# Down-projection of a gated MLP in column parts of 448 and 256 instead of 352 and 352, with the operand's rows closed up and moved by 64 bytes

## The chip, the cores and the metric

The kernel runs on one core of one Trainium2 chip. The metric is the device time of one execution in microseconds; the time given for a kernel is the median of several executions. TensorE (PE) multiplies, VectorE (DVE), ScalarE (ACT) and GpSimd (POOL) do the elementwise work, and SyncE (SP) issues most of the DMAs.

## The reference, cut to what matters

One layer of a streaming encoder for 2048 prompt tokens and 64 sample tokens, model width 1024. The first half is a normalised and modulated projection into a pooling mixer and a matrix-memory recurrence, an output projection and a residual. The second half is the one that is changed here:

```python
h2 = rmsnorm(x, g2) * (1 + sc2) + sh2
up = h2 @ w_up                                  # 1024 -> 2 * 2816
conv = b_conv + sum(w_conv[j] * upp[:, j:j + T] for j in range(3))
a, g = jnp.split(conv, 2, -1)
x = x + gt2 * ((jax.nn.silu(g) * a) @ w_down)   # 2816 -> 1024, the down-projection
y = rmsnorm(x, g_final)
```

All is float32.

## The kernel before, in words

Features lie on the 128 partitions and tokens along the free dimension, so a matmul has a 128x128 block of weights as its stationary operand and a row of tokens as its moving operand. To keep float32 accuracy, each operand is held as two float32r numbers, a rounded high part and the low rest. One product is three matmuls (`PASSES`, L401): high weights by high data, high weights by low data, low weights by high data. Every matmul loads its stationary block anew.

The attention half works in four groups of 512 tokens, the last of them with the 64 sample tokens added (576, in blocks of 256 and 320 columns). Its projections are the matmuls of L416 (data moves) and L970/L1039 (weights move, data stationary).

The MLP half works in three groups of 704 tokens (`fgroups`, `FT` = 704, `FH` = 352). The 22 blocks of 128 inner features are taken in four parts of 5, 5, 6 and 6 (`PARTS`). For each block the up-projection is made by a scheme of seven products on halves of 352 columns (`product`, L1438 to L1447; its matmuls are L1443). Then follow convolution, SiLU and gate, and the result `tg`, 128x704, is split into its high and low part: `split_hi` on ACT (L1558) writes the high part into a tile `av`, `split_lo` on DVE (L1566) the low rest behind it. The tile has 1536 columns.

When the blocks of one part are done, the down-projection of that part runs (`down`, L1699 to L1712, matmuls at L1704): for each of the 8 blocks n of 128 output features, and each block k of the part, three passes, and in each pass one matmul for every column part in `secs`. `down_end` (L1714) adds the sum, scaled, to the residual `x3` on DVE (L1719). There are 3 x 22 x 8 x 3 = 1584 such passes, with two matmuls each.

How `av` lies, before: in all but the last part of the last group ("apart") the tile holds four rows of 384 columns, of which 352 are used: high left, high right, low left, low right. So every moving row of 352 columns starts a multiple of 1536 bytes after the start of the tile. In the block with index 1 of each part the low right row is moved by `NUDGE` = 4 columns, and the split is written in two pieces for that. In the last part of the last group, the tile has two rows of 704, 768 columns apart. There the first three n use the halves 0 to 352 and 352 to 704, and the other five use `ENDS`, 0 to 448 for all five n and then 448 to 704 for all five n, so that the final norm of the first columns can begin early.

In the built program the buffers of streamed weights (`wt`) begin 96 bytes past a multiple of 256 bytes, and so does every 128x128 block in them. The tiles `av` begin 224 bytes past one. In the last part, the weights of the five last n lie in other buffers (`hx`), which begin 224 bytes past a multiple of 256. The data tiles of the attention half (`hl`, `mx`) hold their rows 160 bytes past one.

The order on PE, ACT, DVE and POOL is the program's in this half (a manual schedule); a list of small steps (`todo`, `tick`) puts the elementwise work of the next block between the matmuls. Weights come on SP's queue in the order in which they are used, some units ahead. Accumulators are six banks of PSUM taken in turn, two for each n.

Of the kernel before, what the change touches and what calls it, by code (L numbers as in the profile page):

```python
# [9 lines left out]
F32 = mybir.dt.float32  # L10
F32R = mybir.dt.float32r
AF = mybir.ActivationFunctionType
ALU = mybir.AluOpType
# [12 lines left out]
FT = 704  # L26
FH = FT // 2
NFG = NTOK // FT
NE = 3
EB = 1  # L30
ENDS = ((0, 448), (448, 704))
PARTS = ((0, 5), (5, 10), (10, 16), (16, 22))
EPS = 1e-6
HD = 128
# [7 lines left out]
XR = 384  # L42
XT = 4 * XR
NUDGE, NUDGED = 4, "T1"
# [15 lines left out]
def tile_layer(ctx: ExitStack, tc: tile.TileContext, xT, vecs, cst, rst, rowv, w_mod, w_ada, w_qkou, w_v, w_pool,  # L60
               w_out, w_up, w_down, st_C, st_pool, yT, o_pool, o_C, o_m, o_conv):
    nc = tc.nc
    act, dve, pool, pe = nc.scalar, nc.vector, nc.gpsimd, nc.tensor
# [30 lines left out]
    def scr():  # L94
        return sp.tile([P, TMAX], F32, tag="scr", name="scr")
# [59 lines left out]
    def pair_of(t, row, n):  # L155

        return t[:, :2 * row].rearrange("p (a t) -> p a t", a=2)[:, :, :n]
# [73 lines left out]
    for g in range(NG):  # L231
# [9 lines left out]
        for bi, (lo, hi) in enumerate(o.blks):  # L241
            for (a, b, s) in o.segs:
                l, h = max(lo, a), min(hi, b)
# [59 lines left out]
    for g in range(NFG):  # L303
        for (f0, f1_) in PARTS:
            late = []
# [7 lines left out]
            for i, (n, k) in enumerate(order):  # L313
# [3 lines left out]
                if k % 4 == 0 or (n, c) not in seen:  # L317
                    seen.add((n, c))
                    d = min(c + 4, f1_)
# [6 lines left out]
    class Unit:  # L326

        state = 0
        w = raw = None
# [460 lines left out]
    if True:  # L790
# [110 lines left out]
        h, pb = [], []  # L901
# [422 lines left out]
        for o in groups:  # L1324
# [15 lines left out]
            if o.g == 0:  # L1340
                dve.tensor_copy(M[:, GT + 1:GT + 2], RV[:, 2:3])
                dve.tensor_scalar(out=GH, in0=V[:, V_GH:V_GH + NH], scalar1=0.5, scalar2=None, op0=ALU.mult)
                t = scr()
                nc.sync.dma_start(out=t[:36, :512], in_=cst[:36, NCST + 512:NCST + 1024])
                dve.tensor_copy(E_r.rearrange("p h n -> p (h n)"), t[:36, :512])
                t = scr()
# [34 lines left out]
            h = hn  # L1381
# [74 lines left out]
    class Pair:  # L1456
# [85 lines left out]

        def split_hi(self):
            t = f2.tile([P, XT], F32R, tag="av", name="av", bufs=6)
            self.apart = not (self.o.last and self.f >= PARTS[-1][0])
            if self.apart:
                d = t.rearrange("p (a h t) -> p a h t", a=2, h=2)
                w = NUDGE if self.i == 1 else 0
                self.cuts = [(lambda b, i=i, pa=pa, pb=pb: d[:, b, i, pa + w * b * i:pb + w * b * i], a + 2 * s, b + 2 * s)
                             for (i, pa, pb, a, b, s) in self.o.pieces] if self.o.last or w else [  # L1550
                    (lambda b: d[:, b, :, :FH], 0, FT)]
                self.av[self.i] = lambda b, lo, hi: d[:, b, lo // FH, w * b * (lo // FH):w * b * (lo // FH) + hi - lo]
            else:
                d = pair_of(t, 2 * XR, FT)
                self.cuts = [(lambda b, lo=a, hi=e: d[:, b, lo:hi], a + 2 * s, e + 2 * s) for (a, e, s) in self.o.segs]
                self.av[self.i] = lambda b, lo, hi: d[:, b, lo:hi]
            for cut, a, b in self.cuts:
                act.activation(cut(0), self.of_tg(cut(0), a, b), AF.Copy)  # L1558

        def of_tg(self, like, a, b):  # L1560
            v = self.tg[:, a:b]
            return v.rearrange("p (h t) -> p h t", h=2) if len(like.shape) == 3 else v

        def split_lo(self):
            for cut, a, b in self.cuts:
                dve.tensor_tensor(out=cut(1), in0=self.of_tg(cut(0), a, b), in1=cut(0).bitcast(F32), op=ALU.subtract)  # L1566

    def reload(Bo):
        for nm in BN:
# [103 lines left out]
    for o in fgroups:  # L1673
        Bo = B[o.g]
        for pi, (f0, f1_) in enumerate(PARTS):
            nf = f1_ - f0
            lastp = pi == len(PARTS) - 1
            ends = o.last and lastp
# [51 lines left out]
                if ends:  # L1730
                    act.activation(x3[n][:, lo:hi], x3[n][:, lo:hi], AF.Copy, scale=V[:, V_GF + n:V_GF + n + 1])

            both = ((0, FH), (FH, FT))
            Ws = [Row() for _ in range(NE)]
            pss = []

# [19 lines left out]
            rows = {n: Row() for n in range(NE, KD)}  # L1756
            for secs in [(c,) for c in ENDS] if ends else (both,):
                sums = [(ssum, 0)]
# [94 lines left out]
```

## Time and profile before

| what | value |
|---|---|
| time, median of 3 runs | 2228.41 us (2227.61 to 2228.67) |
| profiled execution, its own time | 2224.26 us |
| its span, first to last instruction | 2222.5 us |
| mean granted TensorE clock | 0.996 |
| PE busy | 2193.2 us (99%) |
| DVE, ACT, POOL busy | 1572.3 us (71%), 1004.6 us (45%), 200.3 us (9%) |
| matmuls of L1443 (seven products) | 5544 |
| matmuls of L1704 (down-projection) | 3168 |

The busy time of an engine is the union of its instructions. A matmul's record shows when it starts and a modelled end; records overlap, because matmuls are pipelined. So the cost of one in a row of matmuls is read from the distance of their starts, which is the busy time of a row of them without gaps divided by their number, not from the mean duration. The chain of waits gives such stretches: "x264" beside a start and a length is a row of 264 matmuls on the path. A count in a window takes in each matmul that touches the window.

### The profile page before, as it was taken

The numbers are of one execution on the slowest core, as the hardware profiler recorded it, in microseconds if no ns is written. First come the engines' busy times: TensorE is split into PE (matmuls) and PEld (weight loads), VectorE is DVE, ScalarE is ACT, GpSimd is POOL, SyncE is SP. The second block draws the span as 40 slices with busy tenths as digits, with TensorE's granted clock in tenths as the row PEclk, the third lists the DMA queues.
The fourth block names the chain that finished last, engine by engine and source line by source line (L and its number), as shares of the span: only waits on it lengthen the run. The fifth ranks groups of instructions, "written<-read, shape, count | busy, mean of one in ns | idle before, by whom it ended". The sixth has DMA issues, their size and how long they took to land.

```text
span 2222.5 us, 37975 instructions
## 1 busy us (share of the span) xinstructions
PE 2193.2 (99%) x13726; PEld 2079.8 (94%) x13726; DVE 1572.3 (71%) x2906; ACT 1004.6 (45%) x1992; POOL 200.3 (9%) x475
## 2 busy tenths in 40 slices
PE   8999999999999999999999999999999999999998
PEld 6888888888899989999999999999999999999998
DVE  5877659567765778687858677677767685757474
ACT  4553334244333446465636344545445353445254
POOL 0010001001000101010000210000001210101012
PEclk9999999999999999999999999999999999999999
DMA  9968986997899476657656865556448554353442
GB/s 367 328 239 270 326 291 225 333 308 246 286 304 302 144 239 208 212 170 267 210 170 215 288 220 197 194 196 203 151 163 281 190 191 159 110 179 121 143 154 81
DMA packets 276444, 493.52 MB, mean 222 GB/s; under 512 B 24952, under 2 KB 103416, under 8 KB 276256
## 3 DMA queue, kind: packets, MB, share of 16 engines
q1 hardware_dynamic: 264480, 463.01, 62.8%
q10 hardware_dynamic: 11776, 28.09, 3.4%
q8 instruction: 108, 1.77, 0.3%
q14 instruction: 80, 0.66, 0.1%
HBM read 382.77 MB, written 108.22 MB: 221 GB/s over the span
## 4 chain that ended last, share of the span: by engine, by line
PE 59%; DVE 1%; DMA 1%; ACT 1%; issue 1%; POOL 0%; POOLq 0%; ACTq 0%; DVEq 0%
PE mm L1443 38%; PE mm L1704 21%; DMA raw<-w_down 1%; DMA wt<-wsum 0%; DVE tg L1431 0%; ACT tg L1426 0%; DVE wt L362 0%; DMA wt<-wsplit 0%; ACT wt L359 0%; DVE y L1656 0%; PE m L1599 0%; ACT av L1558 0%; DVE tg L1541 0%; DVE ta L1431 0%; DVE x L1719 0%
## 5 line engine op out<-in xcount | busy, mean ns | idle before, releaser
L1443 PE MATMUL mm<-hx,wt 128*128 128x352 f32 x5544 | 887.4, 321 | 5.2 <-DVE wt L362 2.7
L1443 PEld LDWEIGHTS mm<-hx,wt 128*128 128x128 f32 x5544 | 881.4, 188 | 6.9 <-DVE wt L362 2.9
L1704 PE MATMUL mm<-av,wt 128*128 128x352 f32 (+2 forms) x3168 | 509.7, 321 | 0.5 <-DVE av L1566 0.3
L1704 PEld LDWEIGHTS mm<-av,wt 128*128 128x128 f32 x3168 | 502.6, 188 | 3.9 <-DVE av L1566 0.9
L416 PE MATMUL mm<-hl,wt 128*128 128x512 f32 (+2 forms) x1920 | 398.2, 359 | 4.6 <-DMA wt<-hl_kept 2.2
L362 DVE TENSOR_TENSOR wt<-raw,wt 128x512 fp32r<-128x512 f32 (+3 forms) x494 | 307.1, 637 | 90.6 <-ACT wt L359 88.0
L416 PEld LDWEIGHTS mm<-hl,wt 128*128 128x128 f32 x1920 | 313.0, 188 | 54.0 <-issue 7.1
L359 ACT ACTIVATE wt<-raw 128x512 fp32r<-128x512 f32 (+3 forms) x494 | 271.4, 570 | 199.6 <-PE mm L1704 85.3
L416 PE MATMUL mm<-mx,wt 128*128 128x512 f32 (+1 forms) x960 | 187.4, 355 | 2.0 <-DVE wt L362 1.6
L1719 DVE SCALAR_TENSOR_TENSOR x<-mm,MOD,x 128x352 f32<-128x352 f32 (+4 forms) x224 | 106.5, 526 | 113.6 <-PE mm L1704 113.5
L416 PEld LDWEIGHTS mm<-mx,wt 128*128 128x128 f32 x960 | 160.2, 190 | 27.3 <-DVE wt L362 1.9
L1431 DVE SCALAR_TENSOR_TENSOR tg<-eg,V,tg 128x704 f32<-128x704 f32 (+1 forms) x132 | 125.7, 952 | 52.3 <-ACT tg L1426 49.9
L362 DVE TENSOR_TENSOR wt<-wt 128x512 fp32r<-128x512 f32 x176 | 121.8, 692 | 41.9 <-ACT wt L359 41.9
L359 ACT ACTIVATE wt<-wt 128x512 fp32r<-128x512 f32 x176 | 109.9, 626 | 66.8 <-DMA wt<-wsum 58.2
L1431 DVE SCALAR_TENSOR_TENSOR ta<-ea,V,ta 128x704 f32<-128x704 f32 (+1 forms) x132 | 125.7, 952 | 7.6 <-ACT ta L1426 5.1
L1566 DVE TENSOR_TENSOR av<-tg,av 128x704 fp32r<-128x704 f32 (+4 forms) x112 | 62.1, 588 | 45.5 <-ACT av L1558 45.2
L1537 ACT ACTIVATE tg<-tg 128x704 f32<-128x704 f32 (+1 forms) x66 | 52.4, 793 | 81.6 <-DVE tg L1431 75.9
L1491 ACT ACTIVATE u<-mm 128x352 f32<-128x352 f32 x66 | 30.5, 463 | 127.5 <-PE mm L1443 92.4
L1451 DVE TENSOR_TENSOR eg<-mm,u 128x352 f32<-128x352 f32 x154 | 70.2, 468 | 23.0 <-ACT u L1506 11.2
L196 DVE SCALAR_TENSOR_TENSOR acc<-raw,CA,acc 128x512 f32<-128x512 f32 x84 | 60.6, 745 | 32.8 <-DMA raw<-w_ada 32.8
L1039 PE MATMUL mm<-wt,hl 128*128 128x256 f32 (+1 forms) x576 | 70.9, 282 | 0.0
L1039 PEld LDWEIGHTS mm<-wt,hl 128*128 128x128 f32 x576 | 69.2, 188 | 1.0 <-issue 0.6
(280 smaller groups left out, 1947.7 us busy)
## 6 DMA issues: line engine op xcount, KB each, us to landing
wt<-hl_kept SPq DMA_DIRECT2D x108, 512.0 KB, 6.1
raw<-w_up SPq DMA_DIRECT2D x198, 256.0 KB, 3.8
wt<-wsum SPq DMA_DIRECT2D x176, 256.0 KB, 3.9
wt<-wsplit SPq DMA_DIRECT2D x88, 512.0 KB, 4.3
raw<-w_down SPq DMA_DIRECT2D x96, 256.0 KB, 3.4
w<-w_up SPq DMA_DIRECT2D x88, 256.0 KB, 5.5
wsum<-w SPq DMA_DIRECT2D x44, 512.0 KB, 4.8
wsplit<-wt SPq DMA_DIRECT2D x44, 512.0 KB, 4.2
```

The costliest lines, as they stand in the source:

```text
L196: dve.scalar_tensor_tensor(out=acc[s], in0=w, scalar=CA[:, k, s:s + 1], in1=acc[s], op0=ALU.mult, op1=ALU.add)
L359: act.activation(u.w[:, 0, :u.n], u.raw[:, :u.n], AF.Copy)
L362: dve.tensor_tensor(out=u.w[:, 1, :u.n], in0=u.raw[:, :u.n], in1=u.w[:, 0, :u.n].bitcast(F32), op=ALU.subtract)
L416: pe.matmul(ps[bi][:, :hi - lo], U[:, a, k % 4 * P:(k % 4 + 1) * P], mv[k][:, b, lo:hi], start=(at == 0 and pi == 0), stop=(k == order[-1] ...
L1039: pe.matmul(ps[ti][:n, :cols], h[4 * kh + k4][:, b, lo:lo + n], U[:, a, k4 % 2 * cols:(k4 % 2 + 1) * cols], start=(kh == 0 and k4 == 0 and ...
L1431: dve.scalar_tensor_tensor(out=t[:, :E], in0=ext[:, j:j + E], scalar=wc(j, f), in1=t[:, :E], op0=ALU.mult, op1=ALU.add)
L1443: pe.matmul(ps[:, :FH], U[:, a, kc * P:(kc + 1) * P], Bo.at(nm, kc, b), start=(first and kc == 0 and pi == 0), stop=(kc == 3 and pi == 2), ...
L1451: dve.tensor_tensor(out=ext[:, d:d + b - a], in0=ps[:, a:b], in1=u[:, a:b], op=ALU.add)
L1537: act.activation(self.tg[:, :E], self.tg[:, :E], AF.Silu)
L1566: dve.tensor_tensor(out=cut(1), in0=self.of_tg(cut(0), a, b), in1=cut(0).bitcast(F32), op=ALU.subtract)
L1704: pe.matmul(ps[i][:, :hi - lo], U[:, a, k % 4 * P:(k % 4 + 1) * P], av[k](b, lo, hi), start=(k == 0 and (a, b) == PASSES[0]), stop=(k == n ...
L1719: dve.scalar_tensor_tensor(out=x3[n][:, a:b], in0=ps[i][:, a - lo:b - lo], scalar=gt2(n, s), in1=x3[n][:, a:b], op0=ALU.mult, op1=ALU.add)
```

## The change

The two rows of `av` are written without a gap, the high part's 704 columns and then the low part's, from column `SIDE` = 16 (64 bytes) of the tile on, in all parts. The split is one piece on each engine, or two in the last group, where the 64 sample tokens follow a gap in `tg`. The down-projection uses the column parts 0 to 448 and 448 to 704 (`ENDS`) everywhere. The nudge in `av` is gone; that in the operand of the seven products stays.

A part of 448 columns is 1792 bytes and a row of 704 is 2816 bytes, both multiples of 256. So all four rows now start at the same place within 256 bytes: in the built program 32 bytes past a multiple, while the streamed weights keep their 96.

```diff
+SIDE = 16
         def split_hi(self):
             t = f2.tile([P, XT], F32R, tag="av", name="av", bufs=6)
-            self.apart = not (self.o.last and self.f >= PARTS[-1][0])
-            if self.apart:
-                d = t.rearrange("p (a h t) -> p a h t", a=2, h=2)
-                w = NUDGE if self.i == 1 else 0
-                self.cuts = [(lambda b, i=i, pa=pa, pb=pb: d[:, b, i, pa + w * b * i:pb + w * b * i], a + 2 * s, b + 2 * s)
-                             for (i, pa, pb, a, b, s) in self.o.pieces] if self.o.last or w else [
-                    (lambda b: d[:, b, :, :FH], 0, FT)]
-                self.av[self.i] = lambda b, lo, hi: d[:, b, lo // FH, w * b * (lo // FH):w * b * (lo // FH) + hi - lo]
-            else:
-                d = pair_of(t, 2 * XR, FT)
-                self.cuts = [(lambda b, lo=a, hi=e: d[:, b, lo:hi], a + 2 * s, e + 2 * s) for (a, e, s) in self.o.segs]
-                self.av[self.i] = lambda b, lo, hi: d[:, b, lo:hi]
+            d = t[:, SIDE:SIDE + 2 * FT].rearrange("p (a t) -> p a t", a=2)
+            self.cuts = [(lambda b, lo=a, hi=e: d[:, b, lo:hi], a + 2 * s, e + 2 * s) for (a, e, s) in self.o.segs]
+            self.av[self.i] = lambda b, lo, hi: d[:, b, lo:hi]
             for cut, a, b in self.cuts:
-                act.activation(cut(0), self.of_tg(cut(0), a, b), AF.Copy)
+                act.activation(cut(0), self.tg[:, a:b], AF.Copy)
...
         def split_lo(self):
             for cut, a, b in self.cuts:
-                dve.tensor_tensor(out=cut(1), in0=self.of_tg(cut(0), a, b), in1=cut(0).bitcast(F32), op=ALU.subtract)
+                dve.tensor_tensor(out=cut(1), in0=self.tg[:, a:b], in1=cut(0).bitcast(F32), op=ALU.subtract)
...
-            both = ((0, FH), (FH, FT))
+            both = ENDS
```

More of the change, by code (lines that the diff above doesn't have):

```diff
@@ L1544, in split_hi @@
             t = f2.tile([P, XT], F32R, tag="av", name="av", bufs=6)
-            self.apart = not (self.o.last and self.f >= PARTS[-1][0])
-            if self.apart:
-                d = t.rearrange("p (a h t) -> p a h t", a=2, h=2)
-                w = NUDGE if self.i == 1 else 0
-                self.cuts = [(lambda b, i=i, pa=pa, pb=pb: d[:, b, i, pa + w * b * i:pb + w * b * i], a + 2 * s, b + 2 * s)
-                             for (i, pa, pb, a, b, s) in self.o.pieces] if self.o.last or w else [
-                    (lambda b: d[:, b, :, :FH], 0, FT)]
-                self.av[self.i] = lambda b, lo, hi: d[:, b, lo // FH, w * b * (lo // FH):w * b * (lo // FH) + hi - lo]
-            else:
-                d = pair_of(t, 2 * XR, FT)
-                self.cuts = [(lambda b, lo=a, hi=e: d[:, b, lo:hi], a + 2 * s, e + 2 * s) for (a, e, s) in self.o.segs]
-                self.av[self.i] = lambda b, lo, hi: d[:, b, lo:hi]
+            d = t[:, SIDE:SIDE + 2 * FT].rearrange("p (a t) -> p a t", a=2)
+            self.cuts = [(lambda b, lo=a, hi=e: d[:, b, lo:hi], a + 2 * s, e + 2 * s) for (a, e, s) in self.o.segs]
+            self.av[self.i] = lambda b, lo, hi: d[:, b, lo:hi]
             for cut, a, b in self.cuts:
[L1558 to L1562, printed above, removed]
+                act.activation(cut(0), self.tg[:, a:b], AF.Copy)
         def split_lo(self):
             for cut, a, b in self.cuts:
-                dve.tensor_tensor(out=cut(1), in0=self.of_tg(cut(0), a, b), in1=cut(0).bitcast(F32), op=ALU.subtract)
+                dve.tensor_tensor(out=cut(1), in0=self.tg[:, a:b], in1=cut(0).bitcast(F32), op=ALU.subtract)
     def reload(Bo):
```

## The prediction

> **What bounds the kernel now.** I read the page's busy rows first, then the chain that ended last in order of time, then windows of single stretches, because only there is the cost of one matmul to be seen.
>
> ```profile
> PE 2193.2 (99%) x13726; PEld 2079.8 (94%) x13726; DVE 1572.3 (71%) x2906; ACT 1004.6 (45%) x1992; POOL 200.3 (9%) x475
> PEclk9999999999999999999999999999999999999999
> PE mm L1443 38%; PE mm L1704 21%; DMA raw<-w_down 1%; DMA wt<-wsum 0%; DVE tg L1431 0%; ACT tg L1426 0%; DVE wt L362 0%; DMA wt<-wsplit 0%; ACT wt L359 0%; DVE y L1656 0%; PE m L1599 0%; ACT av L1558 0%; DVE tg L1541 0%; DVE ta L1431 0%; DVE x L1719 0%
> L1704 PE MATMUL mm<-av,wt 128*128 128x352 f32 (+2 forms) x3168 | 509.7, 321 | 0.5 <-DVE av L1566 0.3
> ```
>
> PE is busy 99% of the span at the full granted clock. The down-projection, L1704, holds 509.7 us of PE and waits only 0.5 us in all of it. So the question is what one matmul costs when the next stands ready, and whether two parts of 448 and 256 columns cost more or less than two of 352. The chain gives the present cost. The columns are start, length and what ran:
>
> ```profile
> 1235.64 41.84 PE mm L1704 x264
> 2082.53 77.93 PE mm L1443 x492
> 2160.47 3.88 PE mm L1704 x24
> ```
>
> 41.84 us for 264 matmuls is 158.5 ns for one and **317.0 ns for a pair**. The seven products, also 352 wide, take 77.93 / 492 = 158.4 ns, with operands in the same place relative to the weights. But the 24 matmuls at the head of the last part, which lie in the other layout, take 161.7 ns: same width, same clock, another place, 3.2 ns more.
>
> **The change part by part.** (1) *The matmuls.* There are 1584 passes with a pair of matmuls each. 1440 of them run in the gapped layout. 54 (three n by six blocks by three passes of the last part) run 352 wide in the ungapped one. The last 90 already use 448 and 256. I call *offset* the distance, modulo 256 bytes, from the beginning of a weight block to that of the moving row: by the program's addresses it is 128 now in the 1440, mixed 128 and 0 in the 54, 0 in the 90, and 192 (32 minus 96) after the change in the first two, 64 (32 minus 224) in the 90. No row shows 448 columns at 192. The widths and offsets that the trace does show:
>
> ```profile
> 2180.00:2196.00 16.00, 16.00 (x81) 1.00 0.12 33
> L1704 PE MATMUL mm<-av,wt 128*128 128x448 f32 x90 | 18.4, 365 | 0.0
> L1704 PE MATMUL mm<-av,wt 128*128 128x256 f32 x90 | 11.5, 285 | 0.0
> 605.00:615.00 10.00, 10.00 (x90) 1.00 1.01 359
> L1039 PE MATMUL mm<-wt,hl 128*128 128x256 f32 x70 | 8.3, 276 | 0.0
> L1039 PE MATMUL m<-wt,hl 128*64 128x256 f32 x20 | 2.6, 276 | 0.0
> 766.00:795.00 29.00, 29.00 (x222) 1.00 0.83 274
> 363.00:397.00 34.00, 34.00 (x150) 1.00 0.81 273
> ```
>
> The first row is the stretch of 448 alone at offset 0 (the fourth column of these window rows is the granted clock, 1.00 in all); rows two and three are its whole groups by shape. In a group without gaps the busy time less one record's modelled length, over the number less one, is the step: 448 takes (18.4 - 0.365) / 89 = **202.6 ns**, and 256, in three stretches, (11.5 - 3 x 0.285) / 87 = **122.4 ns**. Both at offset 0; the pair would be 325.0.
>
> Row four is L1039, 256 columns at **offset 192** (there the streamed weights move and the data stands still; rows five and six say that the window holds nothing else): (10.00 + 0.276) / 90 = **114.2 ns**, 8.2 less than the same width at offset 0, although DMA is busy all the time (share 1.01 against 0.12).
>
> Row seven is L416 in the last attention group, 256 and 320 alternating at **offset 64**: (29.00 + 0.29) / 222 = 131.9 ns at 288 columns on average. Row eight is L416 with 512 columns at the same offset: (34.00 + 0.39) / 150 = 229.3 ns. Through these two goes a line of (229.3 - 131.9) / 224 = 0.435 ns a column and 6.7 ns a matmul. At offset 0 a column costs (202.6 - 122.4) / 192 = 0.418 ns.
>
> So for 448 at offset 192: from below 114.2 + 192 x 0.418 = 194.4, from above the same width at offset 0, 202.6. I take the row of the same offset and the slope of the offset with more rows, 114.2 + 192 x 0.435 = **197.7**. For 256 between 448s: from below 114.2, from above 122.4; I take 114.2, the row with the same offset. The pair is **311.9 ns**, between 308.6 and 325.0.
>
> The sum: 1440 x (311.9 - 317.0) = -7.3 us. 54 x (311.9 - 323.4) = -0.6 us. For the 90 the offset becomes 64, where the line gives 201.5 and 118.0, 5.5 less than 325.0; but the 122.4 has some interruptions by the norm's own matmuls in it, so I take -0.3 us of the -0.5.
>
> Here a rule of the Trainium skill speaks against the change. "SBUF — State Buffer", section "Who interferes with whom", gives TensorE two independent read ports, one for the moving operand and one for the weight load, and names the port pair of VectorE and GpSimd as the only contention. By that the place of the rows could do nothing. The trace does not agree as far as 114.2 and 122.4 ns, or 158.5 and 161.7 ns, differ by place; it does not show which of the two reads gives way.
>
> (2) *The split.* Its pieces, on ACT and DVE:
>
> ```profile
> L1558 ACT ACTIVATE av<-tg 128x704 fp32r<-128x704 f32 x36 | 28.4, 788 | 12.7 <-DVE tg L1541 12.2
> L1558 ACT ACTIVATE av<-tg 128x352 fp32r<-128x352 f32 x32 | 14.9, 491 | 6.2 <-DVE tg L1541 6.1
> L1566 DVE TENSOR_TENSOR av<-tg,av 128x704 fp32r<-128x704 f32 x36 | 32.1, 892 | 26.3 <-ACT av L1558 26.2
> L1566 DVE TENSOR_TENSOR av<-tg,av 128x352 fp32r<-128x352 f32 x32 | 16.1, 525 | 13.7 <-ACT av L1558 13.4
> ```
>
> The eight nudged blocks of the first two groups go from two pieces to one, the 16 of the last group's first three parts from three to two: 24 instructions fewer on each engine. One nudged block saves 2 x 491 - 788 = 194 ns on ACT and 2 x 525 - 892 = 158 ns on DVE. That lies beside PE's work: ACT has 45%, DVE 71%, and PE waits 0.3 us for `av` in the whole run. I count nothing. The bound is the 24 on the path, 24 x 0.35 = -8.4 us, which the 0.3 us of waiting rules out; the stretches where the elementwise chain leads, around a change of group, hold one or two such blocks, at most -0.7 us.
>
> (3) *The evacuation.*
>
> ```profile
> L1719 DVE SCALAR_TENSOR_TENSOR x<-mm,MOD,x 128x352 f32<-128x352 f32 x155 | 83.7, 579 | 106.7 <-PE mm L1704 106.7
> L1719 DVE SCALAR_TENSOR_TENSOR x<-mm,MOD,x 128x448 f32<-128x448 f32 x5 | 3.4, 679 | 4.7 <-PE mm L1704 4.7
> L1719 DVE SCALAR_TENSOR_TENSOR x<-mm,MOD,x 128x192 f32<-128x192 f32 x5 | 2.1, 414 | 2.2 <-PE mm L1704 2.2
> L1719 DVE SCALAR_TENSOR_TENSOR x<-mm,MOD,x 128x288 f32<-128x288 f32 x27 | 13.7, 508 | 0.0
> ```
>
> Two of 352 take 1158 ns; 448 takes 679 and 256 lies between 414 and 508, some 1140 together. The wide one frees its bank 0.1 us later, but six banks turn and one n lasts at least 5 x 3 x 317 ns = 4.8 us, so PE does not come back to it in time to notice. Without that cover it would be 0.1 us at each of 96 ends, +9.6 us. No instruction moves from one engine to another. The order on POOL and on SP's queue is as before, so no DMA is moved past another. A shorter down-projection asks for weights 2% sooner; its DMA share of 0.12 to 0.83 leaves room.
>
> **The sum**: -7.3 - 0.6 - 0.3 = -8.2 us. The profiled execution took 2224.26 us, 1.8 above its span of 2222.5; that gives 2216.1. The median of the runs is 4.15 above it, and on that footing the forecast is **2220.2 us**.
>
> **The rivals.** *As at offset 64.* If what counts is a multiple of 128 bytes, or the mixture of widths, then L416 is the pattern: two matmuls with 704 columns cost 2 x 6.7 + 704 x 0.435 = 319.5, 2.5 more than now. 1440 x 2.5 = +3.6, less 0.2 for the 54 and 0.3 for the 90: +3.1, 2231.5 us. For it: it is this kernel's one alternation of a wide and a narrow part. Against it: 114.2 lies well under the 118.0 of that line.
>
> *The change does not do what it says.* Place has no effect between parts, and 704 columns in two matmuls are 704 columns: 2228.4 us. For it: one line in the number of columns gives equal sums for both ways of cutting. "TensorE: Matmul & The Clock Gate", section "Back-to-back issue gap", has such a line, N/2.4 + 2.5 ns, by which both pairs are an estimated 298 ns; every step here is longer. Against it: the differences by place above.
>
> *Slower: the narrow part lays the weight load bare.* Each matmul needs its weights loaded during the one before.
>
> ```profile
> 1282.23 1.21 PE m L1599 x12
> ```
>
> One-column matmuls step at 1.21 / 12 = 101 ns, so a load takes about that. Under 158.5 ns it has 57 ns to spare, under 114.2 only 13. If a collision of the two reads delays a load by more than that in each narrow part, PE waits for it, and the row for that is 256 between 256s at offset 0: 122.4, with 202.6 for the wide one, which collides too. The pair is then 325.0: 1440 x 8.0 + 54 x 1.6 = +11.6 us, 2240.0 us. It decides from the point where the narrow step passes 317.0 - 197.7 = 119.3 ns. For it: 122.4 is this very instruction. Against it: it was measured at offset 0, which the change leaves.
>
> *Better than forecast.* The wide part has the lower end too, pair 308.6: -12.1 - 0.8 - 0.3 = -13.2 us, 2215.2 us, and lower if 448 keeps the small excess of 256 at 192.
>
> **How the numbers follow.** Forecast 0.46, better 0.06, no effect 0.12, as at offset 64 0.18, slower 0.18. About 0.2%, 4.5 us, is what a measurement of this kernel tells from no change. Of the forecast's 0.46, 0.42 lies beyond that and 0.04 within; of the 0.18 at offset 64, 0.12 lies within and 0.06 above. So faster 0.42 + 0.06 = 0.48, same 0.04 + 0.12 + 0.12 = 0.28, slower 0.06 + 0.18 = 0.24. The range goes from 2215, the lower end of the pair, up to 2237, into the slower rival; some 0.04 is left out below and 0.12 above. The forecast's own range is 2215 to 2225.
>
> **What would show it.** In the chain of waits a piece of 264 matmuls of the down-projection should last 132 x 311.9 = 41.2 us instead of 41.84; 42.2 is the offset-64 rival, 42.9 the slower one. By shape, the mean record of 256 columns should fall from 285 towards 276 ns, and that of 448 stay below 365. The seven products must keep 77.93 us for 492. PE's wait for `av` must stay below 1 us. I am wrong if the pieces of 264 grow, or if they shrink as said and the time doesn't, which would put a wait elsewhere.

## The result

The changed kernel takes 2231.27 us (median of 22 runs, 2227.09 to 2236.2) against 2227.51 us before (22 runs, 2223.05 to 2232.55): a ratio of 1.002, with a 95% interval of 1.0014 to 1.0025. It is slower, by about the 0.2% that I had named as the bound. The forecast was 2220.2 us.

The page of the changed kernel has the same bound as before. Its line numbers have moved: L1692 is the down-projection, L1444 the seven products, L1707 the evacuation.

```profile
span 2227.6 us, 37927 instructions
PE 2198.8 (99%) x13726; PEld 2063.5 (93%) x13726; DVE 1569.1 (70%) x2882; ACT 1002.9 (45%) x1968; POOL 199.3 (9%) x475
L1444 PE MATMUL mm<-hx,wt 128*128 128x352 f32 x5544 | 886.7, 321 | 6.0 <-DVE wt L363 2.0
L1692 PE MATMUL mm<-av,wt 128*128 128x448 f32 (+1 forms) x3168 | 512.8, 322 | 1.5 <-ACT av L1550 0.9
```

The span grew by 5.1 us and the busy time of PE by 5.6. The 24 instructions saved on ACT and on DVE are there (1992 to 1968, 2906 to 2882) and gave nothing. The granted clock is 0.996 in both executions. The busy time of the down-projection's group grew by 3.1 us, and its waits from 0.5 to 1.5 us, all of the 1.5 for `av`. The chain of waits (start, length, what ran) says where:

```profile
1856.69 65.20 PE mm L1444 x408
1926.77 35.52 PE mm L1692 x222
1962.28 77.94 PE mm L1444 x492
2045.97 42.24 PE mm L1692 x264
2171.90 34.98 PE mm L1692 x204
```

The same stretches in the profile of before, with its group of the seven products:

```profile
1852.48 64.63 PE mm L1443 x408
1921.88 35.17 PE mm L1704 x222
2166.33 35.41 PE mm L1704 x204
L1443 PE MATMUL mm<-hx,wt 128*128 128x352 f32 x5544 | 887.4, 321 | 5.2 <-DVE wt L362 2.7
```

A piece of 264 matmuls lasts 42.24 us where it lasted 41.84: **320.0 ns a pair instead of 317.0**, in all five such pieces. The piece of 222 shown here grew in step, from 35.17 to 35.52 us. The last stretch fell, from 35.41 us to 34.98 (-0.4 us), as its rows moved too. Over 1440 pairs 3.0 ns would be +4.3 us. The group's busy time shows less, +3.1 us with the last stretch in it, in part because some shorter pieces of before held a pause that is gone: the pieces of 222 in the first two token groups took 35.35 and 35.37 us, and after the change 35.51.

With the 1.0 us of waits the down-projection makes 4.1 of the span's 5.1 us. The seven products, whose operands weren't touched, take 65.20 us instead of 64.63 in one stretch, but 0.7 us less in all their stretches together, and their waits grew by 0.8 us. No row here says where the last microsecond comes from; these are two single executions. So the larger part of the loss is that the changed matmuls themselves became slower; about a fifth is a longer wait for `av`.

### The profile page after: what moved, and what is told of

It reads as the page before. It is cut to its first block, busy times and chain, and to the rows that moved or that the text cites. A ratio compares the mean times of both kernels' runs of the same rounds, so it can differ in the third digit from the quotient of the medians.

```text
span 2227.6 us, 37927 instructions
## 1 busy us (share of the span) xinstructions
PE 2198.8 (99%) x13726; PEld 2063.5 (93%) x13726; DVE 1569.1 (70%) x2882; ACT 1002.9 (45%) x1968; POOL 199.3 (9%) x475
## 5 line engine op out<-in xcount | busy, mean ns | idle before, releaser
L1444 PE MATMUL mm<-hx,wt 128*128 128x352 f32 x5544 | 886.7, 321 | 6.0 <-DVE wt L363 2.0
L1444 PEld LDWEIGHTS mm<-hx,wt 128*128 128x128 f32 x5544 | 879.4, 188 | 8.3 <-ACT wt L360 2.8
L1692 PE MATMUL mm<-av,wt 128*128 128x448 f32 (+1 forms) x3168 | 512.8, 322 | 1.5 <-ACT av L1550 0.9
L1692 PEld LDWEIGHTS mm<-av,wt 128*128 128x128 f32 x3168 | 484.5, 188 | 26.1 <-ACT av L1550 1.5
L1707 DVE SCALAR_TENSOR_TENSOR x<-mm,MOD,x 128x448 f32<-128x448 f32 (+2 forms) x224 | 106.5, 526 | 115.9 <-PE mm L1692 115.9
L1554 DVE TENSOR_TENSOR av<-tg,av 128x704 fp32r<-128x704 f32 (+1 forms) x88 | 60.5, 708 | 51.5 <-ACT av L1550 51.4
```

The lines of the kernel that those rows point to most:

```text
L1444: pe.matmul(ps[:, :FH], U[:, a, kc * P:(kc + 1) * P], Bo.at(nm, kc, b), start=(first and kc == 0 and pi == 0), stop=(kc == 3 and pi == 2), ...
L1554: dve.tensor_tensor(out=cut(1), in0=self.tg[:, a:b], in1=cut(0).bitcast(F32), op=ALU.subtract)
L1692: pe.matmul(ps[i][:, :hi - lo], U[:, a, k % 4 * P:(k % 4 + 1) * P], av[k](b, lo, hi), start=(k == 0 and (a, b) == PASSES[0]), stop=(k == n ...
L1707: dve.scalar_tensor_tensor(out=x3[n][:, a:b], in0=ps[i][:, a - lo:b - lo], scalar=gt2(n, s), in1=x3[n][:, a:b], op0=ALU.mult, op1=ALU.add)
```

## The experiments

Theory A: the offset of the moving row from the weights sets the price, and 192 is a bad place. Theory B: the cut into unequal parts costs 3 ns a pair wherever the rows lie. Theory C, added after the first four: the starts of the rows must agree modulo more than 256 bytes. Each run is read from its pieces of 264 matmuls, since a single run's time says little about 4 us.

**e1, e2, e3: the changed cut at three other offsets**

```diff
-SIDE = 16
+SIDE = 0     # e1; 32 in e2, 48 in e3
```

> The changed kernel with SIDE = 0: all rows 128 past the weights' place within 256 bytes, the offset of the kernel before, but 448 and 256 wide. If the offset alone sets the price, a pair goes back towards 317 ns and a piece of 264 matmuls to 41.8 us. If it is the cut into 448 and 256, the pair stays at 320 ns and the piece at 42.2 us. If 0 and 128 are alike and both bad, the pair is near 325 ns, 42.9 us.

> The changed kernel with SIDE = 32: offset 0. If the rows of the last stretch before (448 alone 202.6 ns, 256 alone 122.4 ns) carry over to the alternation, the pair is 325 ns and a piece of 264 is 42.9 us, some 7 us more in all than the changed kernel. If the offset does nothing, 320 ns and 42.2 us.

> The changed kernel with SIDE = 48: offset 64, that of the attention half's alternating 256 and 320. By the line through those rows the pair is 319.5 ns, a piece of 264 is 42.2 us, as in the changed kernel. If the offset 192 was a good one and 64 is not, the pair is over 321 ns.

The chain of e1:

```profile
2045.62 42.24 PE mm L1692 x264
```

of e2:

```profile
2046.20 42.24 PE mm L1692 x264
```

and of e3:

```profile
2045.92 42.02 PE mm L1692 x264
```

At offsets 0, 128 and 192 the cut into 448 and 256 costs the same 320.0 ns. At 64 it costs 318.3 (two of the expectations below give it as 318.7). The times are 2230.74, 2230.99 and 2229.53 us, beside 2228.98 for the kernel before. Going back to offset 128 does not bring the 317 back, so theory A alone falls. The sum of 448 alone and 256 alone at offset 0 (325.0) doesn't carry over to the alternation either.

**e4: the old cut at the new offset**

```diff
-                d = t.rearrange("p (a h t) -> p a h t", a=2, h=2)
+                d = t.rearrange("p (a h t) -> p a h t", a=2, h=2)[:, :, :, 16:]
```

> The kernel before with its gapped rows moved by 16 columns: 352 and 352 wide, nudge kept, offset 192 in place of 128. If the offset 192 is the cause of the loss, the pair of 352 rises from 317 to about 320 ns and a piece of 264 from 41.84 to 42.2 us. If the cut into 448 and 256 is the cause, the pair stays within 1 ns of 317, or falls below it, as my forecast's row at offset 192 would have it (about 312 ns, 41.2 us).

Its chain, with the seven products (L1443 here):

```profile
1497.61 77.93 PE mm L1443 x492
1965.68 78.50 PE mm L1443 x492
2049.95 42.26 PE mm L1704 x264
```

Equal halves at offset 192 cost 320.2 ns, so theory B alone falls too. The time was 2235.59 us beside 2228.98, more than the 1440 x 3.2 = 4.6 us of the down-projection. Part of the rest shows in the first and second rows: the seven products, with the same operands in the same places, took 77.93 us in one stretch of 492 and 78.50 in another. In all they are busy for 891.3 us, where they had 887.4 in the profile of before.

**f1: only the cut undone**

```diff
-            both = ENDS
+            both = ((0, FH), (FH, FT))
```

> The changed kernel with the halves 352 and 352 again, rows still closed up from column 16 on: only the cut is undone. The right halves then start at offset 64, the left ones at 192. If the cut into 448 and 256 costs the 3 ns, the pair goes back to 317 ns and a piece of 264 to 41.84 us. If the place of the rows costs them (as e4 says of the gapped rows at 192), it stays at 320 ns, 42.2 us, or lies between 317 and 320, as offset 64 had 318.7.

```profile
2049.21 42.25 PE mm L1692 x264
```

320.1 ns (2233.7 us beside 2229.27): equal halves, one at offset 192 and one at 64, are no better than the new cut.

**f2 and f3: rows alike modulo 1024 bytes, and only the gap back**

```diff
# f2: starts at columns 0, 512, 768 and 1280
+            d = t.rearrange("p (a t) -> p a t", a=2)
...
+            self.av[self.i] = lambda b, lo, hi: d[:, b, lo + (64 if lo else 0):hi + (64 if lo else 0)]
# f3: low row 768 columns behind the high one
-            d = t[:, SIDE:SIDE + 2 * FT].rearrange("p (a t) -> p a t", a=2)
+            d = t[:, :].rearrange("p (a t) -> p a t", a=2)[:, :, SIDE:SIDE + FT]
```

> 448 and 256 wide, but four rows that start at columns 0, 512, 768 and 1280 of the tile, so all four at offset 128 and all on the same place modulo 1024 bytes; more pieces in the split. If what the closed rows lost is that their starts differ modulo 512 bytes (1792 and 2816 bytes are odd multiples of 256), the pair falls to 317 ns and a piece of 264 to 41.84 us. If the cut itself costs, it stays at 320 ns, 42.2 us, as in e1.

> The changed kernel with the low row 768 columns after the high one, so that only the gap between high and low is back: 448 and 256, SIDE 16, offset 192. If the closed gap costs, the pair falls under 319 ns. If not, it stays at 320 ns, a piece of 264 at 42.2 us.

The chain of f2:

```profile
2047.62 42.24 PE mm L1694 x264
```

and of f3:

```profile
2047.77 42.24 PE mm L1692 x264
```

Both stay at 320.0 ns (2232.19 and 2231.17 us beside 2229.27). Theory C falls: neither the closed gap nor the place modulo 512 or 1024 bytes is the cause.

**f4: a milder cut at the old offset**

f3's layout with `SIDE = 0` and `both = ((0, 384), (384, 704))`.

> 384 and 320 wide, low row 768 columns after the high one, SIDE 0: offset 128 and all starts alike modulo 512 bytes, as before, only the cut is another. If unequal cuts cost, the pair is near 320 ns, or between 317 and 320 as the cut is less unequal. If only place counts, it is 317 ns, a piece of 264 41.84 us.

```profile
993.26 36.02 PE mm L1692 x222
2049.28 42.24 PE mm L1692 x264
```

320.0 ns again in the pieces of 264 (2233.53 us beside 2229.27): there 384 and 320 cost what 448 and 256 cost. The pieces of 222 are another matter. Those without a wait took 36.02 to 36.26 us, at least 324.5 ns a pair, where the changed kernel has 35.52 us, 320.0 ns. So this cut has two prices in one execution, with the same offsets in both, and the milder cut is not the cheaper one.

**g1, g2, g3: equal halves without the nudge, and at the remaining offsets**

```diff
-                w = NUDGE if self.i == 1 else 0
+                w = 0                                  # g1
-            t = f2.tile([P, XT], F32R, tag="av", name="av", bufs=6)
+            t = f2.tile([P, XT + 64], F32R, tag="av", name="av", bufs=6)[:, 32:32 + XT]   # g2; 48 in g3
```

> The kernel before without the nudge in av: equal halves at offset 128, every block alike. If the 317 ns are the equal halves at 128 themselves, a piece of 264 stays at 41.84 us or falls by the 8 to 10 ns that each entry into the nudged block shows. If the nudge holds the matmuls in the faster pattern, the pair rises to about 320 ns, 42.2 us, and the lost nudge is the cause of the change's loss.

> The kernel before with its gapped rows moved by 32 columns (in tiles 64 columns longer): equal halves at offset 0, nudge kept. If 128 is the one good place for equal halves, the pair is 320 ns or more (the 24 matmuls at the head of the last part, mixed 0 and 128, had 161.7 ns each, 323 a pair). If only 192 is bad, it stays at 317 ns.

> The kernel before with its gapped rows moved by 48 columns (in tiles 64 columns longer): equal halves at offset 64, nudge kept. The changed kernel's cut had its best pair there, 318.7 ns in e3. If offset and cut add up, equal halves are about 1.5 ns better at 64 than elsewhere: 318.5 ns, a piece of 264 at 42.0 us. If 128 is the one good place, 320 ns, 42.2 us.

The chain of g1:

```profile
2044.21 41.80 PE mm L1704 x264
```

of g2:

```profile
2053.07 42.53 PE mm L1704 x264
```

and of g3:

```profile
2049.73 42.24 PE mm L1704 x264
```

Without the nudge the pair costs 316.7 ns, so its loss is not the cause; it costs 0.3 ns itself. Equal halves at offset 0 cost 322.2 ns in the pieces of 264 (but 320.5 in a piece of 222, which took 35.57 us), and at 64 they cost 320.0. The times are 2228.24, 2238.35 and 2233.25 us, beside 2226.68. **Of all cuts and offsets tried, only equal halves at offset 128 have the 317.** The change gave up both, and f1, e4 and e1 show that giving up either is enough to pay the 3 ns.

g3 has one more reading. In its last stretch the rows lie at offset 192 from the weights there, and 448 and 256 run each by itself, which is the very term that I had to estimate. Its groups by shape:

```profile
L1704 PE MATMUL mm<-av,wt 128*128 128x448 f32 x90 | 18.4, 364 | 0.0
L1704 PE MATMUL mm<-av,wt 128*128 128x256 f32 x90 | 11.0, 280 | 0.0
```

(18.4 - 0.364) / 89 = 202.7 ns for 448 columns, as at offset 0; (11.0 - 3 x 0.28) / 87 = 116.8 ns for 256, against 122.4 at offset 0, interruptions by the norm's matmuls included in both.

**g4: a narrow part below the weight load**

```diff
-            both = ENDS
+            both = ((0, 512), (512, 704))
```

> The changed kernel cut into 512 and 192, SIDE 16. By the line through the attention rows at offset 64, 512 takes 229 ns and 192 takes 90 ns, 319.5 together, as any cut. If a narrow part cannot step faster than a weight load (one-column matmuls step at 101 ns), 192 takes at least 101 ns and the pair at least 328 ns, a piece of 264 at least 43.3 us and some 13 us more in all.

The chain, and the group of the wide part by shape:

```profile
2076.04 45.29 PE mm L1692 x264
```

```profile
L1692 PE MATMUL mm<-av,wt 128*128 128x512 f32 x1494 | 514.4, 416 | 0.1
```

343.1 ns a pair, 23.6 above the line's 319.5, and 2264.21 us beside 2226.68. The wide matmul's record is 416 ns long, where the 512-wide ones of the attention half, in the profile of before, have 400:

```profile
L416 PE MATMUL mm<-hl,wt 128*128 128x512 f32 x1152 | 287.3, 400 | 4.6 <-DMA wt<-hl_kept 2.2 <-DVE wt L362 1.4 <-ACT va L1052 0.9
```

The starts in the trace of g4 say where the time goes. A wide matmul starts 90 ns after a narrow one, as the line says, so the narrow part does step faster than 101 ns. But a narrow one starts 255 ns after a wide one, where the line has 229. The load that runs under a narrow matmul and the next load start 108 ns apart, more than the 90. So the next one starts 21 ns after its wide matmul, where in the changed kernel a load starts 2 to 4 ns after the matmul that covers it. By these starts a narrow part of 192 columns is too short for the load under it, and the delay shows in the step of the wide matmul behind it. At 256 columns the pair shows no such jump.

**h1: rows and weights moved together**

```diff
-        return pair_of(t, 512 if n <= 512 else WN, n)
+        return pair_of(t[:, 16:], 512 if n <= 512 else WN, n)
-                d = t.rearrange("p (a h t) -> p a h t", a=2, h=2)
+                d = t.rearrange("p (a h t) -> p a h t", a=2, h=2)[:, :, :, 16:]
```

> The kernel before with the gapped rows of av and the streamed weights both moved by 64 bytes. In the down-projection the offset is 128 as before, but the rows lie where those of e4 lay (32 past a multiple of 256). The seven products' rows stay, so their offset becomes 64. If what counts is the place of the row relative to the weights, the down-projection's pair is 317 ns (a piece of 264 at 41.8 us) and the seven products rise to about 160 ns a matmul, 78.7 us for 492. If the row's own place counts, the pair is 320 ns (42.25 us) and the seven products stay at 158.4 ns, 77.93 us.

```profile
1965.02 78.72 PE mm L1443 x492
2049.48 41.91 PE mm L1704 x264
```

The rows of the down-projection lie where e4's lay, and yet the pair costs 317.5 ns. The seven products, whose rows were not touched, go from 158.4 to 160.0 ns a matmul, just what g3's halves cost at offset 64. So the place relative to the weights counts, not the place itself. The time was 2234.55 us, beside 2228.67.

**h2: the cheap parts together**

g1 with the changed kernel's closed rows in the last part alone.

> The kernel before without the nudge in av, and with the changed kernel's closed rows from column 16 on in the last part alone. From the traces: 0.2 to 0.3 ns less a pair in 1440 pairs, -0.4 us; the 90 passes of the last stretch 317.8 in place of 322 ns, -0.4 us; the 54 before them 320 in place of 323 ns, -0.2 us. In all -1.0 us, 0.05%, at the edge of what five rounds can tell. If the seven products fall into their slower pattern behind another end of the down-projection, it is slower by up to 5 us.

```profile
2045.99 41.80 PE mm L1704 x264
2171.47 34.98 PE mm L1704 x204
```

Both pieces fell about as expected, from 41.84 to 41.80 and from 35.41 to 34.98 us. The time can't be told from that of before: a ratio of 0.9994, interval 0.9983 to 1.0005.

## Why the prediction was wrong

**What bounds the kernel** was right, and so was the method: PE is bound by the step from matmul to matmul, and the piece of 264 that I named as the sign told the answer: it grew, from 41.84 to 42.24 us, where I had 41.2.

**Step (1), the matmuls, failed in the term "448 at offset 192", 114.2 + 192 x 0.435 = 197.7 ns.** g3 measures 202.7 there. I took a gain seen at 256 columns (8 ns between offsets 0 and 192) and carried it to 448 by a slope; at 448 the two offsets cost the same. The upper end that I had named, the same width at another offset, was the row to take. The second term, 256 at 114.2, came from another group of matmuls, whose data stands still; it is 116.8 in g3. So 5.0 of the 8.1 ns that the pair of 311.9 was short come from the wide part, 2.6 from the narrow one, and 0.5 from the alternation. The starts in the changed kernel's own trace agree: a step is about 203 ns behind a wide matmul and 117 behind a narrow one. The right row for the wide part alone would have given 202.6 + 114.2 = 316.8, no change; it takes both terms to get the loss. Times 1440 the 8.1 ns are 11.7 us, and 2220.2 + 11.7 = 2231.9 against 2231.27. I also never asked whether 317.0 was a price that equal halves have only at that place: I read the 158.5 as the ordinary case, while the runs show it as the exception.

The 54 and the 90 passes of the last part went down, as forecast, but by about half of the 0.9 us: -0.4 us for the 204 matmuls that hold most of them.

**Step (2), the split,** was right in its gain of nothing, but PE's wait for `av` rose from 0.3 to 1.5 us where I had allowed 1. With the same split e1 has 1.1 us of waits and e2 0.7, so part of it changes from execution to execution; no run separates the rest. **Step (3), the evacuation,** was right: no wait for L1707 appears in the down-projection's group. That the measured time lies inside the range I gave is no merit of the sum: the range reached that far for the sake of two rivals.

**The rivals.** "As at offset 64" has the size (319.5 ns, 2231.5 us) for a wrong reason: 64 is the one offset at which the new cut is cheaper (318.3), and 192 does not behave like it. "No effect" is refuted for equal halves by e4, g2, g3 and h1, but nearly holds for 448 and 256, where 0, 128 and 192 cost the same. "Slower", the weight load laid bare, shows at a narrow part of 192 columns (g4) and not at 256; it didn't decide here. The rule of the Trainium skill that spoke against the change ("SBUF — State Buffer", section "Who interferes with whom") gives the moving operand and the weight load independent read ports. By that, place could do nothing. h1 doesn't agree: with the clock at 0.997, moving the weights, with the seven products' rows left in place, took these from 158.4 to 160.0 ns.

**What stays open** is why. That equal halves at offset 128 run at 317, and nearly everything else at 320, is shown, and so is that giving up either the cut or the offset is enough. Why the cut alone costs 3 ns at the good offset, no run explains; a collision between the two reads is a guess that fits h1, and no run shows which read waits.

## What to carry to other kernels

When PE has no gaps, compare the steps of matmuls in pieces of some hundred, and price a new shape only by a row with the same width; a gain seen at one width need not exist at another. Before moving an operand, find out whether the present place is the ordinary case or a good exception: one run that moves only the rows and one that changes only the cut would have shown that each alone loses 3 ns. Where weights are loaded anew for every matmul, beware of narrow parts: one of 192 columns cost 23.6 ns a pair here, one of 256 nothing of the kind.

## What the runs showed of the hardware that I had not expected

In the pieces of 264 the pair of 704 columns comes in few prices: 316.7 to 317.5 ns (equal halves at offset 128: before, g1, h1 and h2), 318.3 (e3) and 320.0 to 320.2 (nine kernels with three cuts and four offsets); only equal halves at offset 0 lie elsewhere among the cuts with no part under 256, at 322.2. The price can differ in shorter pieces of the same execution: f4 has 324.5 ns or more in its pieces of 222.

The seven products have two paces with nothing changed in their operands: 77.93 or 78.5 us for 492 in one and the same execution of e4, and 64.63 or 65.20 for 408 in before and after. The group's busy time in e4 is 3.9 us above that in before. Which stretch gets which pace, and why, was not tried by itself. It blurs the time of a change to one group of matmuls by what happens in another.

A weight load that doesn't fit under a narrow part holds up the next load, and with it the matmul that needs that one: 23.6 ns a pair at 192 columns. The Trainium skill ("TensorE: Matmul & The Clock Gate", section "LDWEIGHTS (loading the stationary operand)") gives a load columns / 1.2 ns, an estimated 107 ns for 128 columns. The trace of g4 agrees: the load under the narrow part, which itself steps by 90 ns, holds the next one back to 108 ns. The narrow part of the changed kernel, 256 columns, steps by 117 and covers a load.
